# A three-stage encoder layer in one kernel: units in their own order, and products that accumulate in PSUM with copies in place of sums

## The chip, the cores and the metric

The kernel runs on one core of one Trainium2 chip. The metric is the device time of one execution in microseconds (us); the number given for a kernel is the median of its runs. A difference of 0.2% (3.9 us) is about what a measurement of this kernel can tell from no change.

## The reference

One encoder layer is applied to a prompt (1024 rows of 1024) and to a sample (512 rows), with the same weights, all in float32.

```python
h = _rmsnorm(x, norm_g)
proj = jnp.einsum('bld,de->ble', h, w_in)
(q, f_fw, f_bw, i, z_a, c_B, c_C, c_x, z_b, g_a, g_b) = jnp.split(proj, SPLIT_POINTS, axis=-1)
o_a = _hgrn2_bidir(q, i, f_fw, f_bw, lb_fw, lb_bw, hnorm_g).astype(x.dtype)
p_a = jnp.einsum('ble,ed->bld', o_a * jax.nn.silu(z_a), w_a)
conv = _centred_short_conv(c_C * c_x, conv_w, conv_b)
p_b = jnp.einsum('ble,ed->bld', c_B * conv * jax.nn.silu(z_b), w_b)
merged = jax.nn.sigmoid(g_a) * p_a + jax.nn.sigmoid(g_b) * p_b
return x + jnp.einsum('bld,de->ble', merged, w_o)
```

A final RMSNorm follows. `_hgrn2_bidir` is a gated linear recurrence over 8 heads of 128, run in both directions, and each of the 11 parts of `proj` is 1024 wide.

## The kernel before, in words

Every float32 operand is split into a high part (ScalarE, "ACT": `s_h`, `w_h`, L63) and a low part (VectorE, "DVE": `s_l`, `w_l`, L64), and each product is three matmuls, high x high, low x high and high x low. Nearly all matmuls on TensorE ("PE") are 128x128 by 128x512.

The stages follow each other in time:

1. Norm and values, to about 109 us.
2. The prompt's projection (L307), to about 872 us. It uses a Strassen-Winograd scheme: a product of 2x2 blocks with seven block products B11, T1, T2, T3, T4, B21, B22 in place of eight, and sums of blocks before and after.
3. The heads, to about 1514 us. The recurrence of each head is done in many small matmuls, and the sample's projections stand between them as *units* of 24 wide matmuls each (L77; a few are L70), so that PE has work while ACT and DVE prepare the small ones. What is left of the units runs to 1580 us.
4. Branch b, from 1580 us: prompt (L823, 336 matmuls), then sample (L77, 192). Branch a from 1709 us, likewise. Each uses the Strassen-Winograd products again, four blocks of 256 output columns for the prompt.
5. The output product from 1825 us (L823, 504 matmuls in six blocks) with the final norm, to the end.

In stage 3 the loop runs over 3 iterations per head: the two halves of the prompt and the sample. In an iteration the *previous* item gets near scores (L450), transposed keys (L499, into the banks "u" of PSUM, of which there are three, copied out by ACT), scores (L450, L484) and contributions (L512, also into "u" banks, copied out by ACT in L513); the current one gets its decays (L434 to L437, a chain between ACT and DVE). When all parts of a group have their contributions, `states` combines them on DVE (L521), `outputs` multiplies them with the queries (L536), and `finish` transposes the result (L550, "u" banks again) and multiplies it with a gate on DVE (L551). The order of the engines is that in which this code is written; it is kept as it is on PE, DVE, ACT and on the SyncE queue ("SP"), which issues all DMAs.

In stages 4 and 5 `two_blocks` makes one block of 256 output rows: `Rows` loads two 512 KB pieces of weights (`w_raw`), `sums` makes the sums S on DVE and splits them into the five buffers `w_h`, `w_l`, and `prod` runs one of the seven products, 12 matmuls into a PSUM bank of its own. DVE adds the products up in SBUF (`plus`, L827), adds a product to the sum and multiplies with the gate `s` (in branch a it also adds branch b's result, `pb`), and stores the result. The gates, `pb` tiles, and the raw operand pieces that `operands` loads (L724) share the pool `io` of seven 512 KB places. The last two operands, B21 and B22, are loaded by `last()`, four pieces for k = 0 to 3, each split twice on ACT and twice on DVE.

The memory of `cs`, a pool on the right side that holds what the heads need, is given to `wk` (S, sums, final gains) only when `order_pe` has closed, behind the last unit.

## Time and profile before

| | |
|---|---|
| median of 3 runs | 1956.26 us (1956.11 to 1957.43) |
| profiled execution | 1956.1 us, span 1954.2 us |
| busy | PE 1918.1 us (98%), DVE 1461.1 us (75%), ACT 940.2 us (48%) |
| matmuls in the trace | 14772 |

The span is the time from the first to the last instruction in the trace. Busy time is summed per engine. A wait is put down to the instruction or DMA that ended it. A wide matmul's row has a duration of 0.39 us, but such matmuls overlap: they start some 0.23 us apart.

### The profile page before, as it was taken

Reading aid. Unit: us, or ns where it says so; the run is one execution under the profiler, and the core shown is the slowest. Engines: PE = TensorE matmul, PEld = TensorE weight load, DVE = VectorE, ACT = ScalarE, POOL = GpSimd, SP = SyncE. Lnnn points to the kernel's source line nnn. Section 1 sums busy time; section 2 is a strip of 40 time slices with the busy share of each in tenths; the row PEclk is TensorE's granted clock in tenths of the full one; section 3 lists DMA queues with packets and bytes.
Section 4 is the critical chain, followed back from the end, with each engine's and each line's share of the span. In section 5 each row is a group of like instructions: output and inputs, shape, how many; then the busy total and the mean of one; then the engine's idle time right before and its main releaser. Section 6 shows DMA issues by size and latency. Waiting matters only on the chain.

```text
span 1954.2 us, 38023 instructions
## 1 busy us (share of the span) xinstructions
PE 1918.1 (98%) x14772; PEld 1615.2 (83%) x14772; DVE 1461.1 (75%) x2423; ACT 940.2 (48%) x1946; POOL 135.8 (7%) x220
## 2 busy tenths in 40 slices
PE   8999999999999999999999999999999999999998
PEld 8988888888888888887888888888888878888786
DVE  6558787878787878785677578878773557899887
ACT  6433443434444343434677577677674333434432
POOL 1000000000000000002122011122110000000000
PEclk8999999999999999999999999999999999999999
DMA  7466676676676767668555655555544965879852
GB/s 214 124 211 236 230 234 235 229 237 226 226 247 217 247 223 245 224 218 318 218 209 189 224 179 198 199 190 205 181 162 159 328 215 189 291 238 304 281 162 86
DMA packets 306436, 427.35 MB, mean 219 GB/s; under 512 B 26192, under 2 KB 178000, under 8 KB 306256
## 3 DMA queue, kind: packets, MB, share of 16 engines
q1 hardware_dynamic: 306256, 424.93, 63.7%
q8 instruction: 116, 1.90, 0.4%
q14 instruction: 64, 0.52, 0.1%
HBM read 254.98 MB, written 169.87 MB: 217 GB/s over the span
## 4 chain that ended last, share of the span: by engine, by line
PE 79%; DVE 8%; ACT 6%; issue 3%; DMA 3%; POOL 1%; SPq 0%; DVEq 0%; POOLq 0%; ACTq 0%
PE pp L307 39%; PE pw L823 13%; PE pp L77 12%; PE pp L201 5%; PE pw L77 3%; PE pp L70 2%; DVE K L436 2%; PE o L536 1%; ACT cat L435 1%; PE sc L450 1%; ACT cat L434 1%; DVE Q L437 1%; PE u L512 1%; POOL rs_o L81 1%; ACT oz L544 1%
## 5 line engine op out<-in xcount | busy, mean ns | idle before, releaser
L307 PE MATMUL pp<-s_h,w_h 128*128 128x512 f32 x1120 | 436.3, 390 | 1.2 <-ACT w_h L63 1.2
L307 PE MATMUL pp<-s_l,w_h 128*128 128x512 f32 x1120 | 436.2, 389 | 0.0
L307 PE MATMUL pp<-s_h,w_l 128*128 128x512 f32 x1120 | 436.2, 389 | 0.0
L77 PE MATMUL pp<-s_h,w_h 128*128 128x512 f32 x632 | 252.5, 400 | 1.2 <-ACT K L132 0.9
L63 ACT ACTIVATE w_h<-w_raw 128x512 fp32r<-128x512 f32 (+1 forms) x204 | 141.3, 693 | 226.4 <-PE pp L307 154.8
L307 PEld LDWEIGHTS pp<-s_h,w_h 128*128 128x128 f32 x1120 | 210.3, 188 | 45.3 <-ACT w_h L63 1.8
L77 PE MATMUL pp<-s_h,w_l 128*128 128x512 f32 x632 | 247.0, 391 | 0.0
L77 PE MATMUL pp<-s_l,w_h 128*128 128x512 f32 x632 | 246.5, 390 | 0.0
L307 PEld LDWEIGHTS pp<-s_h,w_l 128*128 128x128 f32 x1120 | 210.3, 188 | 43.6
L312 DVE TENSOR_TENSOR tmp<-pp,tmp 128x512 f32<-128x512 f32 x240 | 165.3, 689 | 108.2 <-PE pp L307 107.1
L307 PEld LDWEIGHTS pp<-s_l,w_h 128*128 128x128 f32 x1120 | 210.3, 188 | 43.4
L63 ACT ACTIVATE w_h<-w_S 128x512 fp32r<-128x512 f32 x160 | 99.5, 629 | 188.7 <-PE pp L307 85.9
L64 DVE TENSOR_TENSOR w_l<-w_raw,w_h 128x512 fp32r<-128x512 f32 (+1 forms) x204 | 155.7, 764 | 36.0 <-ACT w_h L63 35.7
L823 PE MATMUL pw<-s_h,w_h 128*128 128x512 f32 x392 | 154.1, 393 | 5.5 <-ACT w_h L63 5.5
L823 PE MATMUL pw<-s_h,w_l 128*128 128x512 f32 x392 | 154.4, 394 | 1.8 <-DVE w_l L64 1.8
L823 PE MATMUL pw<-s_l,w_h 128*128 128x512 f32 x392 | 154.0, 393 | 0.0
L434 ACT COPY cat<-K 128x512 f32<-128x512 f32 x168 | 112.2, 668 | 65.8 <-DVE K L436 36.2
L77 PEld LDWEIGHTS pp<-s_h,w_l 128*128 128x128 f32 x632 | 118.7, 188 | 25.5
L77 PEld LDWEIGHTS pp<-s_h,w_h 128*128 128x128 f32 x632 | 118.9, 188 | 24.5 <-ACT K L132 1.3
L77 PEld LDWEIGHTS pp<-s_l,w_h 128*128 128x128 f32 x632 | 119.0, 188 | 22.9
L436 DVE TENSOR_TENSOR K<-K,T 128x512 f32<-128x512 f32 x144 | 110.7, 768 | 30.7 <-ACT cat L434 27.7
L435 ACT COPY cat<-Q 128x512 f32<-128x512 f32 x168 | 112.3, 668 | 39.6 <-DVE Q L437 20.0
(188 smaller groups left out, 3288.0 us busy)
## 6 DMA issues: line engine op xcount, KB each, us to landing
w_raw<-in_w_in SPq DMA_DIRECT2D x80, 512.0 KB, 5.2
ws_d<-w_h SPq DMA_DIRECT2D x160, 256.0 KB, 2.4
ws_d<-w_l SPq DMA_DIRECT2D x160, 256.0 KB, 2.5
w_h<-ws_d SPq DMA_DIRECT2D x79, 512.0 KB, 4.3
w_l<-ws_d SPq DMA_DIRECT2D x79, 512.0 KB, 5.3
fkq_d<-sg SPq DMA_DIRECT2D x48, 256.0 KB, 2.3
v_raw<-in_w_in SPq DMA_DIRECT2D x32, 256.0 KB, 3.4
fkq_d<-sk SPq DMA_DIRECT2D x32, 256.0 KB, 2.4
```

The source lines that it names most:

```text
L63: A.activation(hi, src, AF.Copy)
L64: V.tensor_tensor(lo, src, hi.bitcast(F32), op=ALU.subtract)
L70: T.matmul(out, lhs(k, a), parts[k // 2][b][:, k % 2, :], start=k == 0 and n == 0, stop=k == KT - 1 and n == 2)
L77: T.matmul(out, whl[a][:, k, :], rhs(k, b), start=k == 0 and n == 0, stop=k == KT - 1 and n == 2)
L81: G.tensor_tensor(r, t, neghalf[:, :t.shape[-1]], op=ALU.pow)
L201: T.matmul(pp, B[f"B{k // 4 + 1}{t + 1}"][a][:, k % 4, c * P:(c + 1) * P], parts[k][b], start=k == 0 and m == 0, stop=k == KT - 1 and m == 2)
L307: T.matmul(bank, hl[x][:, k, :], B[b][y][:, k, :], start=k == 0 and i == 0, stop=k == 3 and i == 2)
L312: V.tensor_tensor(out, p, t, op=ALU.add)
L434: A.copy(ap(cat, 0, [[2 * hs, nb], [hs, 2], [1, hs]]), kall)
L435: A.copy(ap(cat, TB, [[2 * hs, nb], [hs, 2], [1, hs]]), qall)
L436: V.tensor_tensor(kall, kall, ap(t, m + 1, [[2, nb], [-m - 1, 2], [0, hs]]), op=ALU.mult)
L823: T.matmul(bank, hl[x][:, c:c + P], O[n][y][:, k, :], start=k == 0 and i == 0, stop=k == 3 and i == 2)
```

## The change

In stage 3 the units are in another order: for each head q, ff, fb, za, cx, cC, cB, zb, and all of gb and ga at the end. `finish` of the prompt and of the sample moves to the third iteration of the next head, around the scores; the sample's `outputs` moves to the second iteration behind contributions and a unit; two units stand at the end of the third iteration and one less in the second.

In stages 4 and 5 a product can continue the bank of an earlier one. B11, T2, T3 and T4 accumulate in one bank, T1 and B22 in another, B21 has its own. ACT copies the bank out three times on the way (c11, u2, u3); what was summed in SBUF is now summed in PSUM, and DVE has 56 additions less, ACT 28 copies more. The next block's B11 is made before the current block's products are done (`begun`), and in the first block `last()`, which loads the operands for B21 and B22, comes behind the next block's `Rows` and B11. `w_raw` has a pool of its own, `rp`; `cs` closes with the heads, and gates of left-over units go to `io`. In the changed file L500, L513, L537, L551, L552 are the former L499, L512, L536, L550, L551, and L730, L901, L904, L935 the former L724, L883, L886, L916.

```diff
         p0st.close()
+        rp = outer.enter_context(tc.tile_pool(name="rp", bufs=1, side="right", reuse_waits="tile"))
         cs = right.enter_context(tc.tile_pool(name="cs", bufs=1, side="right", reuse_waits="tile"))
         wp = st.enter_context(tc.tile_pool(name="wpp", bufs=1, side="right", reuse_waits="tile"))
...
-                ahead = [cs.tile([P, 1024], F32R, name=f"a_{x}") for x in "hl"]
+                ahead = [rp.tile([P, 1024], F32, name="w_raw", bufs=2) for _ in range(2)]
                 for a, z in enumerate(ahead):
-                    load(z.rearrange("p (k c) -> p k c", c=P).bitcast(F32), ws_d[SPLIT["q"], a])
+                    load(z.rearrange("p (k c) -> p k c", c=P), ws_d[SPLIT["q"], a])
...
+        gate_tile = lambda: cs.tile([P, TB], F32, name="sg", bufs=2)
...
-                s = cp.tile([P, TB], F32, name="sg", bufs=2)
+                s = gate_tile()
...
-        later = [narrow(n, h) for h in range(NH) for n in ("cx", "cC", "cB", "zb", "gb")]
-        later.insert(8, wide(1))
-        later += [narrow("ga", h) for h in range(NH)]
         units = []
         for h in range(NH):
-            units += [narrow(n, h) for n in ("q", "ff", "fb", "za")] + [wide(0)] * (h == 0) + later[4 * h:4 * h + 4]
-        units += later[4 * NH:]
+            units += [narrow(n, h) for n in ("q", "ff", "fb", "za")]
+            units += [wide(h // 2)] * (h in (0, 2)) + [narrow(n, h) for n in ("cx", "cC", "cB", "zb")]
+        units += [narrow(n, h) for n in ("gb", "ga") for h in range(NH)]
...
-        prev, to_output, to_finish = None, None, None
+        prev = None
         for i in range(len(order) + 1):
+            h, m = divmod(i, 3)
...
             if prev:
                 near_scores(prev)
                 transpose_keys(prev)
-            if to_output:
-                outputs(to_output, 0)
+            if m == 0 and h:
+                outputs(groups[h - 1], 0)
             if cur:
                 decays(cur)
                 if cur.b == 0:
                     values(cur.g)
-                    if cur.g.n == 8:
-                        cur.g.zg = gtile("zgp", [2 * TB])
-                        load(cur.g.zg, zg_d[cur.g.h])
             unit()
+            if m == 2 and h:
+                finish(groups[h - 1])
             if prev:
                 scores(prev)
+            if m == 2:
+                if h:
+                    finish(sample[h - 1].g)
+                groups[h].zg = gtile("zgp", [2 * TB])
+                load(groups[h].zg, zg_d[h])
+            if prev:
                 contributions(prev)
             unit()
-            if to_finish:
-                finish(to_finish)
-            if to_output:
-                outputs(to_output, 1)
-            if i % 3 < 2:
+            if m == 0 and h:
+                outputs(groups[h - 1], 1)
+            if m == 1 and h:
+                outputs(sample[h - 1].g, 0)
+            if m != 1:
                 unit()
-            to_finish, to_output = to_output, None
             if prev and len(prev.g.done) == len(prev.g.tbs):
-                to_output = prev.g
                 states(prev.g)
             prev = cur
+        outputs(sample[NH - 1].g, 0)
         unit()
-        outputs(to_output, 0)
-        if to_finish:
-            finish(to_finish)
-        unit()
-        finish(to_output)
+        finish(groups[NH - 1])
+        finish(sample[NH - 1].g)
         left.close()
+        right.close()
 
 
 
 
         qp, io = opened(outer, "qp", bufs=1), opened(outer, "io", bufs=7)
         ps = opened(outer, "psc", bufs=1, space=PSUM)
+        wk = opened(outer, "wk", bufs=1, side="right")
+        gate_tile = lambda: io.tile([P, TB], F32, name="io")
...
         def raw_block(src):
-            raw = io.tile([P, 1024], F32, name="w_raw", bufs=2)
+            raw = rp.tile([P, 1024], F32, name="w_raw", bufs=2)
...
-        def products(O, r, srcs, use):
-
-
-
+        def products(O, last, r, srcs, use):
+
+
+            def prod(hl, half, n, bank=None):
+                start = bank is None
+                if start:
+                    bank = ps.tile([P, TB], F32, name="pw", bufs=5)
+                for k in range(4):
+                    for i, (a, b) in enumerate(PASSES):
+                        c = half * TB + k * P
+                        T.matmul(bank, hl[a][:, c:c + P], O[n][b][:, k, :],
+                                 start=start and k == 0 and i == 0, stop=k == 3 and i == 2, skip_group_check=True)
+                return bank
+
+            def copied(bank):
+                c = wk.tile([P, TB], F32, name="c", bufs=6)
+                A.copy(c, bank)
+                return c
+
+            def begun(r):
+                r.x = prod(r.f, 0, "B11")
+                r.c11 = copied(r.x)
+
+            begun(r)
             i = 0
             while r.raws:
-                r = two_blocks(O, r, partial(use, i), i > 0, partial(srcs, i + 1))
+                if i:
+                    r.sums(0)
+                    r.sums(1)
+                ahead = Rows(srcs(i + 1))
+                if i == 0:
+                    y = prod(r.s12, 0, "T1")
+                prod(r.s12, 1, "T2", r.x)
+                u2 = copied(r.x)
+                if i == 0:
+                    ahead.first()
+                    begun(ahead)
+                    last()
+                else:
+                    y = prod(r.s12, 0, "T1")
+                prod(r.s34, 0, "T3", r.x)
+                u3 = copied(r.x)
+                use(i, 0, 0, prod(r.f, 1, "B21"), r.c11)
+                use(i, 1, 1, y, u3)
+                prod(r.last, 0, "T4", r.x)
+                use(i, 1, 0, r.x, None)
+                if i and ahead.raws:
+                    ahead.first()
+                    begun(ahead)
+                prod(r.s34, 1, "B22", y)
+                use(i, 0, 1, y, u2)
+                r = ahead
                 i += 1
-
-        def two_blocks(O, r, use, early, later):
-            def prod(hl, half, n):
-                bank = ps.tile([P, TB], F32, name="pw", bufs=5)
-                for k in range(4):
-                    for i, (x, y) in enumerate(PASSES):
-                        c = half * TB + k * P
-                        T.matmul(bank, hl[x][:, c:c + P], O[n][y][:, k, :], start=k == 0 and i == 0, stop=k == 3 and i == 2)
-                return bank
-
-            def plus(out, p, t):
-                V.tensor_tensor(out, p, t, op=ALU.add)
-
-            c11, c12, c21 = (wk.tile([P, TB], F32, name="c", bufs=6) for _ in range(3))
-            if early:
-                r.first()
-            A.copy(c11, prod(r.f, 0, "B11"))
-            if early:
-                use(0, 0, c11, prod(r.f, 1, "B21"))
-                r.sums(0)
-            plus(c12, prod(r.s12, 1, "T2"), c11)
-            if early:
-                r.sums(1)
-            ahead = Rows(later())
-            plus(c21, prod(r.s34, 0, "T3"), c12)
-            p5 = prod(r.s12, 0, "T1")
-            plus(c12, p5, c12)
-            use(1, 1, c21, p5)
-            use(1, 0, c21, prod(r.last, 0, "T4"))
-            if not early:
-                use(0, 0, c11, prod(r.f, 1, "B21"))
-            use(0, 1, c12, prod(r.s34, 1, "B22"))
...
-            def use(i, m, t, c, more):
+            def use(i, m, t, u, more):
                 m += 2 * i
-                u = wk.tile([P, TB], F32, name="sum", bufs=2)
-                V.tensor_tensor(u, more, c, op=ALU.add)
+                if more is not None:
+                    V.tensor_tensor(more, u, more, op=ALU.add)
+                    u = more
                 finish_block(m, t, s[m], u)
...
             r = prepared(srcs)
-            products(last(), r, srcs, use)
...
             def block(m, t, s, u):
-                V.tensor_tensor(u, u, s[:, t, :], op=ALU.mult)
-                V.tensor_tensor(s[:, t, :], u, pb[m][:, t, :], op=ALU.add)
+                V.tensor_tensor(s[:, t, :], u, s[:, t, :], op=ALU.mult)
+                V.tensor_tensor(s[:, t, :], s[:, t, :], pb[m][:, t, :], op=ALU.add)
...
                 V.tensor_tensor(x, c, x, op=ALU.add)
-                V.tensor_tensor(x, more, x, op=ALU.add)
+                if more is not None:
+                    V.tensor_tensor(x, more, x, op=ALU.add)
...
         order_pe.close()
-        right.close()
-        wk = opened(outer, "wk", bufs=1, side="right")
         fg = wk.tile([P, D], F32, name="fg")
         load(fg, w["final_g"].to_broadcast([P, D]))
-        branch_b_prompt(lambda: last_operands(O, take(0, 1), rows))
+        branch_b_prompt(O, lambda: last_operands(O, take(0, 1), rows))
```

PE in the third iteration of a head and the beginning of the next, before: L512 are the contributions that complete the prompt's group, L550 the transposes of the sample's finish, L536 the prompt's outputs. The rows left out are the 24 wide matmuls of one unit.

```order
L512 MATMUL u<-v_11694,kT 128x128 x7
...
L550 MATMUL u<-ident,oz 128x128 x4
L450 MATMUL sc<-q,kd 32x32 x16
L450 MATMUL sc<-cat 32x32 x48
L499 MATMUL u<-ident,K 128x128 x6
L536 MATMUL o<-v_11694,pt 128x128
L536 MATMUL o<-us_12173,Q 128x128
```

The same place after; the first gap is one unit, the second two.

```order
L500 MATMUL u<-ident,K 128x128 x7
...
L551 MATMUL u<-ident,oz 128x128 x8
L451 MATMUL sc<-cat 32x32 x48
L485 MATMUL sc<-cat 64x64 x8
L551 MATMUL u<-ident,oz 128x128 x4
L513 MATMUL u<-v_11697,kT 128x128 x7
...
L451 MATMUL sc<-q,kd 32x32 x16
L451 MATMUL sc<-cat 32x32 x48
L500 MATMUL u<-ident,K 128x128 x6
L537 MATMUL o<-v_11697,pt 128x128
L537 MATMUL o<-us_12152,Q 128x128
```

A second unit has come between contributions and outputs, all twelve transposes of the finishes have moved ahead of the contributions, and before them the eight stand behind a unit of their own.

The SyncE queue at the start of branch a, before: L724 loads the pieces of oz_p for B21 and B22, L883 and L886 load gates and pb tiles (here those of block 0 and the first of block 1), L762 loads weights, L916 stores a finished tile.

```order
L886 DMA io_18637<-pb_p_77 128x1024 [waits DMAHW5_49,DMAHW3_49]
L883 DMA io_18639<-sga_p_81 128x1024 [waits DMAHW6_49,DVE_49]
L886 DMA io_18641<-pb_p_77 128x1024 [waits DMAHW0_49,DVE_49]
L724 DMA io_18668<-oz_p_75 128x1024 [waits DMAHW7_49,DMAHW2_49]
...
L724 DMA io_18674<-oz_p_75 128x1024 [waits DMAHW5_49,DMAHW3_49]
L724 DMA io_18680<-oz_p_75 128x1024 [waits DMAHW2_49,DVE_49]
L724 DMA io_18686<-oz_p_75 128x1024 [waits DMAHW6_49,DMAHW0_49]
L883 DMA io_18727<-sga_p_81 128x1024 [waits DMAHW5_49,DMAHW1_49,DVE_49]
...
L916 DMA m_p_79<-io_18639 128x1024
```

After: L901 and L904 load gates and pb tiles, L935 stores a finished tile, L730 loads the pieces of oz_p.

```order
L904 DMA io_18648<-pb_p_77 128x1024 [waits DMAHW5_49,DMAHW3_49]
...
L901 DMA io_18650<-sga_p_81 128x1024 [waits DMAHW6_49]
L768 DMA w_raw_18809<-in_w_a 128x8x128 [waits DMAHW0_49,DMAHW1_49,DVE_49,Activation_49]
L904 DMA io_18652<-pb_p_77 128x1024 [waits DVE_49]
L935 DMA m_p_79<-io_18602 128x1024 [waits DMAHW2_49]
L730 DMA io_18704<-oz_p_75 128x1024 [waits DMAHW2_49]
L730 DMA io_18710<-oz_p_75 128x1024 [waits DMAHW4_49,DMAHW3_49,DVE_49]
L730 DMA io_18716<-oz_p_75 128x1024 [waits DMAHW5_49,DMAHW4_49,DVE_49]
L768 DMA w_raw_18811<-in_w_a 128x8x128 [waits DVE_49]
L730 DMA io_18722<-oz_p_75 128x1024 [waits DMAHW7_49,DMAHW5_49,DVE_49]
```

The loads of oz_p stood ahead of block 1's gates and of every store; now they stand behind all eight tiles of blocks 0 and 1 and behind the first store.

DVE ahead of branch b, before: S are the sums of block 0's weights; the splits `s_l` of operands are those that run along the last units and, the eight of them, those of B21 and B22.

```order
L64 TENSOR_TENSOR s_l<-io,s_h 128x512 x2
L64 TENSOR_TENSOR w_l<-w_raw,w_h 128x1024
L64 TENSOR_TENSOR s_l<-io,s_h 128x512 x8
L793 TENSOR_TENSOR S<-w_raw 128x512
L789 TENSOR_TENSOR S<-w_raw 128x512
L794 TENSOR_TENSOR S<-S,w_raw 128x512
```

After, where L552 is the last gate multiplication of the heads.

```order
L552 TENSOR_TENSOR oz<-u,zg 128x512
L799 TENSOR_TENSOR S<-w_raw 128x512
L795 TENSOR_TENSOR S<-w_raw 128x512
L800 TENSOR_TENSOR S<-S,w_raw 128x512
L796 TENSOR_TENSOR S<-w_raw,S 128x512
L64 TENSOR_TENSOR s_l<-io,s_h 128x512
```

The sums have moved from behind the operands' splits to the end of the heads.

## Rows read from the trace of the kernel before

**Rows 1.** The page, busy time of each engine, share of the span and instructions.

```profile
PE 1918.1 (98%) x14772; PEld 1615.2 (83%) x14772; DVE 1461.1 (75%) x2423; ACT 940.2 (48%) x1946; POOL 135.8 (7%) x220
```

**Rows 2.** Windows by stage: us, busy time (instructions) by engine, PEclk, DMA share, GB/s.

```profile
core 0: us, PE busy (x) PEld busy (x) DVE busy (x) ACT busy (x) POOL busy (x), PEclk, DMA share, GB/s
...
872.00:1514.00 642.00, 628.29 (x8718) 532.48 (x8717) 445.27 (x802) 417.76 (x1070) 118.81 (x192) 1.00 0.57 204
...
1580.00:1709.00 129.00, 124.66 (x543) 102.42 (x543) 103.82 (x149) 48.24 (x66) 0.00 (x0) 0.99 0.71 231
1709.00:1825.00 116.00, 116.00 (x513) 96.14 (x512) 105.01 (x156) 42.35 (x58) 0.00 (x0) 1.00 0.83 274
```

**Rows 3.** Waits of PE: engine, line, what for; us in total, times, longest us.

```profile
PE pw L823 <- ACT w_h L63: 5.5, 3, 4.0
PE u L550 <- ACT us L513: 5.4, 4, 1.7
PE o L536 <- DVE us L521: 4.3, 6, 1.6
```

**Rows 4.** Timeline, PE from 955 to 968: start, us, form, xcount [wait].

```profile
955.18 1.06 PE L450 MATMUL sc<-cat 128*32 128x32 f32 x96
956.17 0.69 PE L484 MATMUL sc<-cat 128*64 128x64 f32 x16
...
966.00 0.39 PE L536 MATMUL o<-v,pt 128*128 128x128 f32 x2
967.21 0.49 PE L536 MATMUL o<-us,Q 128*128 128x128 f32 x2 [0.82 <-DVE us L521]
967.53 0.39 PE L536 MATMUL o<-v,pt 128*128 128x128 f32 x2
```

**Rows 5.** Timeline from 1306 to 1313, PE's and DVE's part of a finish.

```profile
1306.59 0.60 PE L550 MATMUL u<-ident,oz 128*128 128x128 f32 x4
...
1308.88 0.66 PE L550 MATMUL u<-ident,oz 128*128 128x128 f32 x4 [1.69 <-ACT us L513]
...
1309.29 0.48 PE L77 MATMUL pp<-s_h,w_h 128*128 128x512 f32 x1
...
1309.60 0.40 PE L77 MATMUL pp<-s_l,w_h 128*128 128x512 f32 x1
...
1312.16 1.27 DVE L551 TENSOR_TENSOR oz<-u,zgp 128x512 f32<-128x512 f32 x2
```

**Rows 6.** Timeline from 1582 to 1592, the start of branch b.

```profile
1582.54 0.39 PE L823 MATMUL pw<-s_h,w_l 128*128 128x512 f32 x1
...
1583.86 0.69 DVE L793 TENSOR_TENSOR S<-w_raw 128x512 f32<-128x512 f32 x1
...
1591.52 0.39 PE L823 MATMUL pw<-s_h,w_l 128*128 128x512 f32 x1
```

**Rows 7.** Tile oz_p from 1690 to 1760: issues on SyncE, first and last start.

```profile
L724 SPq DMA_DIRECT2D io<-oz_p x4: 319/320/320, 1702.8 to 1713.7; - x4
...
DMA to landing us min/median/max: 3.3/4.4/5.4
```

**Rows 8.** Tile m_p from 1690 to 1790, the stores of L916.

```profile
DMA to landing us min/median/max: 3.3/5.1/7.0
```

**Rows 9.** Timeline from 1831 to 1836, the start of the output stage.

```profile
1831.25 0.50 PE L823 MATMUL pw<-s_h,w_h 128*128 128x512 f32 x1 [1.02 <-ACT w_h L63]
...
1834.12 0.61 ACT L63 ACTIVATE w_h<-w_raw 128x512 fp32r<-128x512 f32 x1
1834.18 0.69 DVE L945 TENSOR_TENSOR io<-c,io 128x512 f32<-128x512 f32 x1
1834.79 1.22 DVE L64 TENSOR_TENSOR w_l<-S,w_h 128x1024 fp32r<-128x1024 f32 x1
1835.92 0.69 DVE L64 TENSOR_TENSOR w_l<-w_raw,w_h 128x512 fp32r<-128x512 f32 x1
```

**Rows 10.** Timeline of the end; the last matmul starts at 1945.75.

```profile
1947.27 0.68 DVE L946 TENSOR_TENSOR io<-pw,io 128x512 f32<-128x512 f32 x1
```

More of the change, by code (lines that the diff above doesn't have):

```diff
@@ L587, in prepare @@
                 if (name, h) == ("q", 0):
-                    return [z.rearrange("p (k c) -> p k c", c=P) for z in ahead]
+                    return [z.rearrange("p (k c) -> p k c", c=P).bitcast(F32R) for z in ahead]
                 return parts_from(ws_d[SPLIT[name] + h], (KT, P))
@@ L871, in branch_b_sample, with branch_prompt @@
                 store(pb_x[1][j], s)
-        def branch_prompt(name, last, finish_block, pb=None):
+        def branch_prompt(name, O, last, finish_block, pb=None):
             s = {}
@@ L886, in srcs, with branch_b_prompt @@
                         load(pb[j].rearrange("p a b -> p (a b)"), pb_x[0][j])
[L888 removed]
+            def use(i, m, t, u, more):
                 m += 2 * i
[L890 to L891 removed]
+                if more is not None:
+                    V.tensor_tensor(more, u, more, op=ALU.add)
+                    u = more
                 finish_block(m, t, s[m], u)
             r = prepared(srcs)
[L895 to L897 removed]
+            products(O, last, r, srcs, use)
+        def branch_b_prompt(O, last):
             left_of = {}
@@ L904, in block, with branch_a_prompt @@
                     store(pb_x[0][m], s.rearrange("p a b -> p (a b)"))
-            branch_prompt("w_b", last, block)
-        def branch_a_prompt(last):
+            branch_prompt("w_b", O, last, block)
+        def branch_a_prompt(O, last):
             pb = {}
             def block(m, t, s, u):
-                V.tensor_tensor(u, u, s[:, t, :], op=ALU.mult)
-                V.tensor_tensor(s[:, t, :], u, pb[m][:, t, :], op=ALU.add)
+                V.tensor_tensor(s[:, t, :], u, s[:, t, :], op=ALU.mult)
+                V.tensor_tensor(s[:, t, :], s[:, t, :], pb[m][:, t, :], op=ALU.add)
                 left_of[m] = left_of.get(m, 0) + 1
@@ L918, in branch_a_prompt @@
             left_of = {}
-            branch_prompt("w_a", last, block, pb)
+            branch_prompt("w_a", O, last, block, pb)
         def branch_a_sample(blocks, act):
@@ L929, in branch_a_sample, with output @@
                 store(m_x[1][j], s)
-        def output(last):
+        def output(O, last):
             xt, ss, halves = {}, {}, {}
@@ L957, in output @@
             r = prepared(srcs)
-            products(last(), r, srcs, use)
+            products(O, last, r, srcs, use)
         FIRST, LAST = ("B11", "T1", "T2", "T3", "T4"), ("B21", "B22")
@@ L994, in trunk_kernel @@
         branch_b_sample(blocks, act)
-        branch_a_prompt(lambda: last_operands(O, take(2, 4), rows))
+        branch_a_prompt(O, lambda: last_operands(O, take(2, 4), rows))
         rows = lambda k: w["w_o"][k * P:(k + 1) * P, :]
@@ L1002, in trunk_kernel @@
         branch_a_sample(blocks, act)
-        output(lambda: last_operands(O, take(5, 6), rows))
+        output(O, lambda: last_operands(O, take(5, 6), rows))
 def _masks():
```

5 lines of the change are left out of this document (1 added, 4 removed).

## Prediction

> **What bounds the kernel now.** The page comes first: TensorE (PE) is busy for 1918.1 of 1954.2 us [rows 1], so the time is a fixed stream of matmuls plus the holes in it. The windows by stage say where the holes are: 13.7 us in the 642 us of the heads stage, 4.3 us at branch_b's prompt part, none from 1709 to 1825, where 513 wide matmuls take 116.00 us, 0.226 us each [rows 2]. PE's own waits name what ends the holes [rows 3]. Every term below is therefore a hole that closes or opens on PE; the 56 additions that leave VectorE (DVE) count only where PE waits for DVE. The profiled execution is 1956.1 us against a median of 1956.26, so the sum is made on 1956.1 and needs no correction.
>
> **The heads stage, what closes.** Six times the prompt outputs (L536) wait for the states that L521 makes, 4.3 us in all [rows 3]. Before, one unit of 24 wide matmuls, the last four transposes of a finish, and the near scores and key transposes stand between the contributions (L512) and these outputs; after, two units and no transposes. One unit more is 24 x 0.226 = 5.4 us, and the longest wait is 1.6 us, so all six should go. Four times the second half of the eight output transposes (L550) waits for a "u" bank that ScalarE (ACT) empties with L513, 5.4 us in all; at 1308.88 PE stands for 1.69 us for the copies of the contributions just ahead [rows 3, 5]. After, the eight transposes stand a whole unit behind the key transposes, and the banks that they take were emptied before or are being emptied by two short copies during that unit. A stop costs a little more than its wait: the step from 966.00 to 967.21 is 1.21 us, the next one 0.32, an excess of 0.89 for a wait of 0.82 [rows 4]. Ten stops at about 0.1 each make it 4.3 + 5.4 + 1.0 = 10.7 us.
>
> **The heads stage, what opens.** After, the contributions (L513) follow the transposes closely and take two banks that now hold transposed outputs, until DVE has multiplied them with the gate (0.64 us each, two in 1.27 [rows 5]). Between the eight transposes and the contributions PE has 48 + 8 score products and four more transposes: 0.99 (955.18 to 956.17), 0.69 and 0.60 at most [rows 4, 5], some 2.2 us less overlaps. If DVE is free, the first product is done 0.64 us behind the first four transposes and nothing waits; DVE may be about 1.9 us late. What DVE has queued ahead there is the decay chain of the next block, which the key copies and six cat copies on ACT pace, and the wide unit in between (5.4 us) covers nearly all of it. Before, PE found DVE late by up to 1.6 us at the states [rows 3]. I put 1.5 us on the seven places together; nothing and 10 us are the ends (0 or 1.4 us each). Seven fewer changes from small to wide matmuls, 0.09 us each (1309.29 to 1309.60 is such a first step, 0.31 against 0.23 [rows 5]), give 0.6 us back.
>
> **branch_b's start.** From the matmul at 1582.54 to that at 1591.52 there are twelve steps, which take 8.98 us instead of 2.72: 6.3 us are lost [rows 6]. Most is one hole right behind 1582.54: the sums S could start only at 1583.86, because their space was the gate pool's, which closed with the last gate. Some steps behind the hole are slower, which the 6.3 us include. After, the pool closes with the heads, DVE makes S some 66 us before it is needed, and all weights that the first three products take are split while the last units run. B21 and B22 now come from operands loaded behind the last gate's store, of which the fourth waits for the first's space: 1 us for that (0.3 to 2). So 6.3 - 1.0 = 5.3 us close.
>
> **branch_a's start, where a hole opens.** Here the order on the SyncE queue decides. Before, the four loads of oz_p that feed B21 and B22 are issued from 1702.8 to 1713.7 [rows 7], and PE has no hole from 1709 on [rows 2]. After, blocks 0 and 1 both ask for their gate and pb tiles first: 8 tiles, and the io pool has 7. The eighth (L904) waits until DVE has finished block 0's first tile, and the oz_p loads stand behind it. Six of the seven places then hold tiles that need B21 or B22 or block 1, so the four loads go one after the other through one place: each waits for the four splits of the one before it, and the first waits for the store of the finished tile.
>
> The times, from branch_a's first matmul: T4 ends after 76 matmuls, at 17.2 us; a multiplication and an addition on DVE (0.69 each when alone [rows 9]) make 18.6, the eighth load and the store's issue 19.3. A store of m_p lands after 5.1 us in the median, a load of oz_p after 4.4 [rows 7, 8]: 24.4 and 28.8. The first split ends at 29.4 (0.61 on ACT [rows 9]); PE, which has eight products to do first, has been waiting since 96 x 0.226 = 21.7, so a hole of 7.7 us. Two splits on ACT and one more on DVE end 2.0 us after a landing, so each of the next three rounds lasts 6.4 us: the last piece lands at 48.0 and its last split ends at 50.0. (Between the splits of the third and the fourth piece DVE has seven other operations, 6 x 0.61 + 1.13 = 4.8 us back to back [rows 9]; these just fit beside the load.) A PE without holes would be there after 168 matmuls, at 38.1: 11.9 us. Behind the last hole some steps are slow. At branch_b the twelve steps lose 6.3 us, of which the long wait is 4.0 [rows 3]; of the other 2.3, a second wait and the slow steps, I take 1.4 for the steps and add it once. It also covers DVE's queue, 13 operations (8.5 us) ahead of a split that PE takes 33 matmuls (7.5 us) later. I take 13.3 us. The ends come from the shortest and longest of these transfers (3.3 and 3.3; 7.0 and 5.4 [rows 7, 8]). With 3.3 the third piece's last split ends at 38.5, DVE's seven operations and the last two splits follow, and 44.6 is 6.5 behind, 7.9 with the slow steps; with 7.0 and rounds of 7.4 it is 55.9, 19.2. After the block the stream is as dense as before and nothing gives this back.
>
> The Trainium skill (DMA: Bandwidth & Descriptors, "Anatomy of one DMA — SWDGE (gpsimd) path") has a DMA cost about 2.0 us plus its bytes at 436 GB/s, fitted to DMAs that GpSimd issues, which for 512 KB is an estimate of 3.2 us. By it the hole would be about the small end, and the time about 1950; the medians of this trace are 4.4 and 5.1, and only its shortest transfers agree.
>
> **The rest of the products.** In the steady state each bank rests for at least one product (12 x 0.226 = 2.7 us) for the ACT copy (a pass over 128x512 takes ACT 0.61 [rows 9]) and for the next weights' split; nothing opens. The output stage starts with the same wait for m_p's rows; one more sum on DVE stands ahead of the one whose split PE awaits at 1831.25 [rows 9], and the next block's B11 comes a little before its rows: 0.6 us (0 to 2). At the end two additions follow the last product instead of one (1947.27 [rows 10]): 0.6 us.
>
> **The sum.** -10.7 + 1.5 - 0.6 - 5.3 + 13.3 + 0.6 + 0.6 = -0.6 us: 1955.5 us.
>
> **The rivals.**
> 1. The hole at branch_a is short: the queues are nearly empty while PE stands still, so each transfer takes 3.3 us. For it: the shortest rows; against it: the loads of weights for block 2 and the stores of block 0 fall in the same stretch. The hole is 7.9, the time 1950.1; with no new wait in the heads, 1948.6. Faster.
> 2. The contributions in the heads wait for DVE: place, the first L513 behind each finish; it opens from a lateness of 1.9 us on, and with 1.4 us at seven places the time is 1955.5 - 1.5 + 10 = 1964; from 0.9 us each on it is slower. For it: DVE is at 445 of 642 us in that stage and the order gives one iteration a unit less than it had [rows 2]; against it: the iteration that was shortest before was shorter still. Slower. The long end of branch_a's hole (19.2) alone gives 1961.4.
> 3. The states stay late although the outputs come 5 us later, because the gate multiplications now stand ahead of them on DVE, so the change does not do what it does on paper there: +4.3 to +5, 1960.
>
> **How the numbers follow.** A measurement of this kernel can tell 0.2%, 3.9 us, from no change: faster is below 1952.3, slower above 1960.2. My forecast holds with 0.42, rival 1 with 0.33, rival 2 or the long hole with 0.17, rival 3 with 0.08, half of it on either side of 1960.2. So faster 0.33, same 0.46, slower 0.21. The range runs from 1948, just beyond rival 1 with clean heads, to 1963, nearly to rival 2; the likeliest case alone is 1952 to 1960.
>
> **What would show it.** In the profile after: no wait of the outputs for states and none of the transposes for ACT's copies; the heads stage 8 to 11 us shorter; no hole at branch_b's first T product; at branch_a the oz_p loads issued one by one, 5 to 7 us apart, from about 24 us behind its first matmul, and four holes on PE ended by their splits, the first near 7 us, 8 to 19 in sum; the clock below full in that stretch. The prediction is wrong if those loads are issued earlier, if PE finds other products to do meanwhile, or if the heads stage gets holes at L513.

## The result, and the profile after

The changed kernel takes 1977.01 us in the median of four runs (1974.79 to 1978.62), the kernel before 1956.19 beside it: a ratio of 1.0104 (95% interval 1.0091 to 1.0116). The profiled execution of the changed kernel has a span of 1975.6 us, 21.3 more than the one of before. The forecast was 1955.5 with a range to 1963, so it was wrong.

The page after, busy time of each engine, which answers to [rows 1]:

```profile
PE 1927.0 (98%) x14772; PEld 1622.2 (82%) x14772; DVE 1431.5 (72%) x2367; ACT 957.4 (48%) x1974; POOL 142.8 (7%) x220
```

DVE has its 56 instructions less and ACT its 28 more; the work on PE is the same 14772 matmuls, 7032 of them wide ones of 128x128 by 128x512. Where the 21.3 us are is seen when the span is cut at the first matmul of each stage. The heads run here from the end of the prompt's projection to branch b's first matmul. "Output" reaches from its first matmul to the end; a wait of that first matmul counts to branch a's sample part.

| us | before | after | difference | predicted |
|---|---|---|---|---|
| heads and left-over units | 697.86 | 710.63 | +12.8 | -9.8 |
| branch b, prompt | 82.44 | 76.20 | -6.2 | -5.3 |
| branch a, prompt | 76.16 | 88.82 | +12.7 | +13.3 |
| branch a, sample | 44.17 | 46.25 | +2.1 | +0.6, the output's first wait |
| output to the end | 127.90 | 128.18 | +0.3 | +0.6, the tail |

What is left, 43.5 us of branch b's sample part and the stages before the heads, differs by under 0.5. The two large terms behind the heads came within 1 us. The heads alone are off by 22.6.

Waits of PE after; columns as in [rows 3].

```profile
PE u L513 <- DVE oz L552: 14.1, 7, 2.4
PE pw L824 <- ACT s_h L63: 5.6, 2, 5.3
PE pw L824 <- ACT w_h L63: 3.8, 2, 2.6
...
PE u L513 <- ACT us L514: 2.5, 1, 2.5
```

The two waits of [rows 3] that were to close, transposes for ACT (5.4) and outputs for states (4.3), are gone from the list. In their place the contributions (L513) stand seven times for DVE's gate multiplication (L552), 2.0 us each, and once for ACT's own copy.

The window of the heads, as in [rows 2]:

```profile
872.00:1514.00 642.00, 621.97 (x8648) 529.02 (x8647) 449.40 (x805) 414.89 (x1053) 126.96 (x191) 0.98 0.57 199
```

In a stretch of the same length PE is busy 6.3 us less and makes 70 matmuls fewer, and its mean granted clock has gone from 1.00 to 0.98 of 2.4 GHz. DVE and ACT are busy within 1% of what they were. So nothing is busier; somebody is late. One of the seven places, on the timeline from 1100 to 1116:

```profile
1100.18 1.23 DVE L417 SCALAR_TENSOR_TENSOR Q<-q,F 128x1024 f32<-128x1024 f32 x1 [17.06 <-PE o L537]
...
1101.60 1.39 POOL L81 TENSOR_TENSOR rs_o<-sso,neghalf 128x4 f32<-128x4 f32 x1 [21.92 <-DVE sso L542]
...
1103.02 1.14 ACT L545 ACTIVATE oz<-o,rs_o 128x128 f32<-128x128 f32 x4 [1.12 <-POOL rs_o L81]
...
1104.04 0.29 ACT L459 ACTIVATE near<-sc 128x128 f32<-128x128 f32 x1
...
1105.03 0.92 ACT L436 COPY cat<-Q 128x512 f32<-128x512 f32 x1
...
1107.64 1.03 PE L551 MATMUL u<-ident,oz 128*128 128x128 f32 x8
...
1111.95 1.28 DVE L552 TENSOR_TENSOR oz<-u,zgp 128x512 f32<-128x512 f32 x2
...
1112.69 2.04 PE L513 MATMUL u<-v,kT 128*128 128x128 f32 x14 [1.82 <-DVE oz L552]
```

The transposed outputs are in their banks from 1108.7 on, but DVE takes them only at 1111.95: the decay chain (L437, L438) stands ahead on it. The chain is late because it passes back and forth between DVE and ACT, and ACT, from 1101.19 to 1104.04, copies one piece of it, stands 1.12 us for GpSimd's `rs_o` and then scales four outputs. It also began late: the place that it needs for `Q` came back only with the sample's outputs (17.06 us idle on DVE, ended by L537). At the other six places DVE stands less than 0.8 us there, while ACT stands 1.1 to 1.7 us for `rs_o` at all seven. Two suspects, then: ACT's wait for GpSimd, and the late return of `Q`.

Branch a's start. SyncE's timeline from 1722 to 1756, loads of weights left out:

```profile
1731.25 0.32 SPq L904 DMA_DIRECT2D io<-pb_p  x1
1731.62 0.43 SPq L935 DMA_DIRECT2D m_p<-io  x1
1736.74 11.99 SPq L730 DMA_DIRECT2D io<-oz_p  x3
...
1753.58 0.32 SPq L730 DMA_DIRECT2D io<-oz_p  x1
```

The tile oz_p from 1700 to 1760, from issue to landing:

```profile
DMA to landing us min/median/max: 3.1/3.2/4.5
```

PE's timeline from 1733 to 1755, its waits for splits of these pieces:

```profile
1740.59 0.80 PE L824 MATMUL pw<-s_h,w_h 128*128 128x512 f32 x1 [5.32 <-ACT s_h L63]
...
1747.11 0.73 PE L824 MATMUL pw<-s_h,w_h 128*128 128x512 f32 x2 [0.32 <-ACT s_h L63]
```

Before, the four loads were issued from 1702.8 to 1713.7, around the first matmul of that part [rows 2, 7]. Now the first goes out 24.4 us behind branch a's first matmul (1712.30), the second at 1741.89, the third at 1748.42: one by one, 5 to 6.5 us apart.

### The profile page after: what moved, and what is told of

Read it like the earlier page. It is cut to its first block, busy times and chain, and to the rows that moved or that the text cites. A ratio compares the mean times of both kernels' runs of the same rounds, so it can differ in the third digit from the quotient of the medians.

```text
span 1975.6 us, 37915 instructions
## 1 busy us (share of the span) xinstructions
PE 1927.0 (98%) x14772; PEld 1622.2 (82%) x14772; DVE 1431.5 (72%) x2367; ACT 957.4 (48%) x1974; POOL 142.8 (7%) x220
## 4 chain that ended last, share of the span: by engine, by line
PE 80%; DVE 7%; ACT 4%; issue 4%; DMA 4%; POOL 1%; SPq 0%; DVEq 0%; POOLq 0%; ACTq 0%
PE pp L308 39%; PE pp L77 16%; PE pw L824 11%; PE pp L201 5%; PE pw L77 2%; DVE Q L438 2%; PE o L537 2%; PE u L513 2%; ACT cat L436 1%; PE sc L451 1%; DVE K L437 1%; DMA io<-in_w_o 1%; DMA w_raw<-in_w_a 1%; POOL rs_o L81 1%; ACT oz L545 1%
## 5 line engine op out<-in xcount | busy, mean ns | idle before, releaser
L308 PEld LDWEIGHTS pp<-s_l,w_h 128*128 128x128 f32 x1120 | 210.2, 188 | 43.5
L438 DVE TENSOR_TENSOR Q<-Q,T 128x512 f32<-128x512 f32 x144 | 111.2, 772 | 27.1 <-ACT cat L436 25.3
```

Of the source, the lines that this page charges most:

```text
L308: T.matmul(bank, hl[x][:, k, :], B[b][y][:, k, :], start=k == 0 and i == 0, stop=k == 3 and i == 2)
L438: V.tensor_tensor(qall, qall, ap(t, 1, [[2, nb], [m - 1, 2], [0, hs]]), op=ALU.mult)
```

## The experiments

Each run is timed beside the kernel before on the same chip; ratios are to that kernel, with 95% intervals. The table cuts their profiled executions as above.

| us | heads | branch b | branch a | a, sample | output | median | ratio |
|---|---|---|---|---|---|---|---|
| e1_fourth_q | 699.8 | 76.2 | 88.3 | 45.1 | 127.6 | 1966.44 | 1.0041 (1.0026 to 1.0056) |
| e2_outputs_back | 688.2 | 76.2 | 88.3 | 46.0 | 127.1 | 1955.70 | 0.9990 (0.9980 to 0.9999) |
| e3_last_first | 711.2 | 76.4 | 82.8 | 43.5 | 126.6 | 1968.15 | 1.0057 (1.0039 to 1.0074) |
| e4_loop_before | 694.2 | 76.2 | 88.4 | 47.7 | 127.8 | 1961.23 | 1.0018 (1.0009 to 1.0027) |
| e5_both_mended | 688.0 | 76.4 | 81.4 | 43.5 | 128.4 | 1944.57 | 0.9931 (0.9914 to 0.9947) |
| e6_fourth_q_no_rs | 684.5 | 76.2 | 88.7 | 47.8 | 127.9 | 1950.47 | 0.9965 (0.9952 to 0.9978) |
| e7_no_rs_three_q | 684.5 | 76.2 | 88.5 | 46.8 | 128.4 | 1951.73 | 0.9976 (0.9967 to 0.9985) |
| e8_sums_in_sbuf | 688.9 | 76.2 | 76.2 | 43.8 | 127.6 | 1940.60 | 0.9913 (0.9898 to 0.9928) |
| e9_first_block_sums | 688.0 | 76.2 | 76.3 | 43.5 | 131.8 | 1942.61 | 0.9923 (0.9910 to 0.9937) |
| e10_late_scaling | 684.9 | 76.2 | 88.3 | 46.1 | 128.2 | 1951.42 | 0.9972 (0.9961 to 0.9983) |
| e11_sums_late_scaling | 706.1 | 76.2 | 76.2 | 46.1 | 127.3 | 1962.91 | 1.0024 (1.0014 to 1.0033) |
| e12_sums_decays_first | 684.8 | 76.2 | 76.2 | 46.3 | 127.5 | 1937.07 | 0.9892 (0.9874 to 0.9910) |

**e1: a fourth place for Q.**

```diff
-            k.Q = Q = gtile("Q", [2, TB], 3)
+            k.Q = Q = gtile("Q", [2, TB], 4)
```

> One edit in the changed kernel: the scaled queries Q get a fourth place in place of three. Theory A (the decay chain of the sample cannot begin before the sample's outputs of the head before have given back its Q, and these outputs now stand at the end of the second iteration; the gate multiplications stand behind that chain on VectorE, and the contributions wait for them): VectorE no longer stands still in the second iteration, the waits of L513 for L552 fall from 14.1 us to below 3, and with the slow steps behind them the time falls by 15 to 22 us, to 1955 to 1962. Theory B (the chain between VectorE and ScalarE is simply longer than the cover, wherever it begins): the waits stay above 8 us and the time above 1971. Theory C (ScalarE is late, since the outputs' normalisation and its wait for GpSimd stand ahead of the chain's copies): as B, since the order on ScalarE is not touched.

Some of the loss goes (heads -10.8), but PE still waits for L552, 11.0 us in five waits: more than theory A has, and the time lies between the bands. ACT now stands longer for GpSimd at such a place: its row at 1169.01 waits 3.91 us for `rs_o`. What the fourth place changes isn't shown: DVE still stands 15.21 us for L537 ahead of L417 at 1094.6.

**e2: the sample's outputs back at the start of the iteration.**

```diff
+            if m == 1 and h:
+                outputs(sample[h - 1].g, 0)
             if cur:
                 decays(cur)
...
-            if m == 1 and h:
-                outputs(sample[h - 1].g, 0)
```

> One edit in the changed kernel: the sample's outputs go back to where they were in the second iteration, right behind the transposed keys, still in the iteration before the finish. Theory A (Q's place): Q is given back early again, the waits of L513 for L552 fall below 3 us, the time to 1955 to 1962. Theory B (the chain is too long in any case): waits above 8 us, time above 1971. Theory C (ScalarE late through the outputs' normalisation): falls like A, so that this run and the one with a fourth Q tell A and C apart together.

The heads take 9.7 us less than before, where the prediction's terms for them sum to 9.8, and the waits at L513 are 2.2 us in five, where it had put 1.5 on seven:

```profile
PE u L513 <- DVE oz L552: 2.2, 5, 0.7
```

So all of the heads' loss comes from the new place of one step, and what else is new there does what it was forecast to do. The move takes back both suspects at once.

**e3: B21's and B22's loads ahead of the next block's.**

```diff
+                if i == 0:
+                    last()
                 ahead = Rows(srcs(i + 1))
...
                     begun(ahead)
-                    last()
```

> One edit in the changed kernel: in each first block the loads of the operands for B21 and B22 are asked for before block 1's rows, gates and pb tiles, as in the kernel before. The theory that the eight gate tiles in seven places cause branch_a's hole: branch_a's prompt part takes 76 to 78 us in place of 88.8, and the time falls by 11 to 13 us, to 1964 to 1966. Rival (the hole comes from the new order of the products, which needs B21 early): it stays above 6 us and the time above 1970.

Neither side of the expectation is met. Branch a gains 6.0 us, not the whole 12.7, and a new wait of PE for ACT's copy (c, L830) of 4.9 us appears.

**e4: the loop of before, the new order of the units.** The heads' loop is that of the diff's minus lines; all else stays changed.

> The changed kernel with the heads' loop of the kernel before (outputs, finish and the number of units in their old places); the new order of the units and all of the products stay. If the whole loss of the heads stage (12.8 us) comes from the loop: the heads stage is as long as before to within 2 us and the time is 1963 to 1966. If the order of the units costs something by itself, the time is above 1968.

The heads take 694.2, 3.7 less than before and 16.5 less than after: neither the units' order nor the pools cost anything there; the loop does. Heads and time are a little below what was expected.

**e5: e2, with `last()` ahead of the block's first product.**

```diff
+            last()
             begun(r)
...
                     begun(ahead)
-                    last()
```

> The changed kernel with the sample's outputs back behind the transposed keys and, in each first block, the operands for B21 and B22 asked for before the first product. If branch_a's hole comes from the queue for the seven places alone: branch_a's prompt part takes 76 to 77 us in place of 88.3, the output stage starts 2 us sooner too, and the time is 1940 to 1943, below both kernels. Rival (the early use of B21 and the copies on ScalarE make a hole by themselves, as the 82.8 us with the loads merely moved ahead of block 1 suggest): branch_a stays above 80 us and the time above 1946.

Branch a still lacks 5.2 us, and the time lies between the bands of the two theories. What is there, on the timeline of e5 from 1694 to 1700:

```profile
1694.20 0.63 ACT L63 ACTIVATE s_h<-io 128x512 fp32r<-128x512 f32 x1 [4.87 <-DMA io<-oz_p]
...
1698.20 1.15 ACT L63 ACTIVATE s_h<-io 128x512 fp32r<-128x512 f32 x2 [1.90 <-DMA io<-oz_p]
...
1699.26 0.56 ACT L830 COPY c<-pw 128x512 f32<-128x512 f32 x1
...
1699.88 0.50 PE L824 MATMUL pw<-s_h,w_h 128*128 128x512 f32 x1 [3.28 <-ACT c L830]
```

B11 was done near 1694, and T2, which continues its bank, could have started at 1696.4. The copy of the bank stands on ACT behind splits that stand for loads.

**e6 and e7: ACT doesn't wait for GpSimd.** Both leave out the scale by `rs_o`; e6 has four places for Q, e7 three.

```diff
-                    A.activation(oz[:, c, :], p[:, c, :], AF.Copy, scale=r[:, c:c + 1])
+                    A.activation(oz[:, c, :], p[:, c, :], AF.Copy, scale=1.0)
```

> The changed kernel with a fourth place for Q, and the recurrence's outputs are copied without their scale (the normalisation by rs_o is left out of the copy, so that ScalarE does not wait for GpSimd there; GpSimd still makes it). Theory C for what the fourth Q left (ScalarE stands for GpSimd's rs_o with the key copies and the chain's copies behind it): the waits of L513 for L552 fall from 11.0 to below 3 us, the heads from 699.8 to 688 to 692, the time to 1955 to 1959. Theory B (the chain is too long by itself): the waits stay above 7 us and the time above 1963.

> The changed kernel with three places for Q as it has, and the outputs copied without their scale (as in the run with a fourth Q and no scale, the normalisation is left out of the copy). If both causes lie one behind the other: the waits of L513 for L552 fall from 14.1 to 4 to 10 us, the heads from 710.6 to 695 to 704. If Q's place alone set the chain's start, they stay above 12 us; if the scale alone did, they fall below 3 us and the heads to 690.

Both take 684.5 us in the heads, and neither has a wait at L513. This is less than e6 was expected to reach, and e7 refutes what I held by then, that both causes act in series: with ACT free, the late Q costs nothing.

**e8: e5 with the products of before.** `products`, `two_blocks` and branch a's and b's sums are those of the diff's minus lines, with `last()` ahead of the first product; the wider pools of the change stay.

> The changed kernel with the sample's outputs back behind the transposed keys, and with the products of the kernel before (each in a bank of its own, sums on VectorE in SBUF, operands loaded first); the early closing of the gate pool stays. If the accumulation in PSUM gives PE nothing and branch_b's gain is that of the early closing: branch_b's prompt part takes 76 to 77 us, branch_a's 76 to 77, and the time is 1940 to 1945. If the accumulation or the earlier B11 is what closed branch_b's hole: branch_b takes above 79 us.

Branch a is back at 76.16, and on ACT the same copy of B11 stands in the same place (at 1698.64, behind four splits); here T2 has a bank of its own, and nobody waits for it. Branch b is as fast without accumulation, and the tail behind the last matmul's start is 8.49 us again instead of 9.21.

**e9: e5, but the first block adds up on DVE.**

```diff
-                prod(r.s12, 1, "T2", r.x)
-                u2 = copied(r.x)
                 if i == 0:
+                    u2 = plus(prod(r.s12, 1, "T2"), r.c11)
                     ahead.first()
                     begun(ahead)
+                    p = prod(r.s34, 0, "T3")
+                    u3, more = plus(p, u2), plus(p, u2)
...
```

> As e5_both_mended, but in the first block of each stage T2, T3 and T4 get banks of their own and DVE adds them up, so that no product of that block waits for ACT's copy of B11; T1 and B22 still share a bank, and all later blocks accumulate as before. If branch_a's remaining 5.2 us are the wait of T2 for that copy, which stands on ACT behind the splits of B21's and B22's first two pieces, branch_a's prompt part is 76.2 to 77.0 us, PE has no wait there for ACT c L830, and the time is 1939.5 to 1941.5. If accumulation costs something else (banks, the order of the next block's B11), branch_a stays at 79 to 82 and the time above 1942.5. What the later blocks' accumulation is worth is this time less that of e8_sums_in_sbuf (1940.6): 0 to +1 by the theory, the longer tail alone.

Branch a takes 76.3, so its 5.2 us were T2's wait for the copy with the slow steps behind it. The total is 1.1 above that theory's band and 2.0 above e8: in the output stage a hole of 3.2 us opens, where the next block's B11, now the fourth product, waits for the split of rows that have just landed:

```profile
1823.14 1.06 ACT L63 ACTIVATE w_h<-w_raw 128x1024 fp32r<-128x1024 f32 x1 [1.45 <-DMA w_raw<-m_p]
...
1824.25 0.79 PE L824 MATMUL pw<-s_h,w_h 128*128 128x512 f32 x1 [3.24 <-ACT w_h L63]
```

**e10: after, with the sample's scaling copies behind the next decays.** Nothing is left out, and Q comes back as late as in the changed kernel. The sample's copies are kept in a list and written later; the prompt's stay where they were:

```diff
-                for c in range(CPB):
-                    A.activation(oz[:, c, :], p[:, c, :], AF.Copy, scale=r[:, c:c + 1])
+                waiting.append((oz, p, r))
...
                     values(cur.g)
+            scaled()
             unit()
```

> The changed kernel, with the sample's outputs in their new place, but ACT's four scaling copies of those outputs (the ones that stand for GpSimd) are written behind the next iteration's decays, among the key copies and the chain. Nothing is left out. Q comes back as late as in the changed kernel. If ACT standing for GpSimd ahead of the key copies and the chain is the cause, the heads take 684 to 689 us and the time is 1950 to 1955, with under 3 us of waits at L513's line. If Q's late return or the place itself is the cause, the heads stay above 700 and the time above 1965. If the scaled outputs now come late for their transposes, a wait of the finish's transposes for ACT opens instead, 1 to 2 us at seven places, 1958 to 1965.

The heads take 684.9. The same place as above, on the timeline from 1093 to 1106 (L551, L558 and L559 are the former L545, L551 and L552):

```profile
1093.10 1.22 DVE L417 SCALAR_TENSOR_TENSOR Q<-q,F 128x1024 f32<-128x1024 f32 x1 [17.06 <-PE o L537]
...
1094.69 0.90 ACT L436 COPY cat<-Q 128x512 f32<-128x512 f32 x1
1095.46 0.31 ACT L459 ACTIVATE near<-sc 128x128 f32<-128x128 f32 x1
1095.94 0.37 ACT L551 ACTIVATE oz<-o,rs_o 128x128 f32<-128x128 f32 x1 [0.17 <-POOL rs_o L81]
...
1100.56 1.03 PE L558 MATMUL u<-ident,oz 128*128 128x128 f32 x8
...
1102.34 1.28 DVE L559 TENSOR_TENSOR oz<-u,zgp 128x512 f32<-128x512 f32 x2
...
1103.62 1.73 PE L513 MATMUL u<-v,kT 128*128 128x128 f32 x14
```

Counted from L417, which waits the same 17.06 us, the transposes start after 7.46 us in both kernels. But the chain's first copy of Q now runs at 1.6 instead of 4.85, DVE is at the gate after 9.24 instead of 11.77, and L513 has no wait. In the whole run one is left at that line:

```profile
PE u L513 <- DVE oz L559: 0.4, 1, 0.4
```

**e11 and e12: the best of both.** Both are e8 with the sample's outputs at the changed kernel's place. In e12 the sample's copies are written as in e10. In e11 the prompt's are moved too, and the sample's are written just behind the key transposes, ahead of the decays; its expectation below describes them wrongly.

> e8_sums_in_sbuf with the sample's outputs back in the place of the changed kernel and all scaling copies on ACT, the prompt's too, behind the decays. By the theory the heads come down from 688.9 to the 684.5 that they took without the scale, and the time from 1940.6 to 1936 (1935 to 1938). If the copies come late for the transposes of the finish, 1940 to 1945.

> e8_sums_in_sbuf with the sample's outputs in the changed kernel's place and its scaling copies behind the next iteration's decays, as in e10_late_scaling and unlike e11_sums_late_scaling, where two of the four copies still stood on ACT ahead of the copy of the near scores. By the theory it takes e10's heads (684.9) and e8's rest: 1940.6 - (688.9 - 684.9) = 1936.6 (1935 to 1939). If e10's gain depended on something other than ACT's order, the heads are 688 or more and the time 1940 or more.

e12 came out as expected, 1937.07 us, and has the lowest median of all; the 3.5 us to e8 are less than the 3.9 that a measurement can tell, but the heads go the same way (684.8 against 688.9). e11 lies 25 us above its range. ACT in e11 at such a place, from 1103 to 1106 (its line 551 is the changed kernel's L545):

```profile
1103.25 0.63 ACT L551 ACTIVATE oz<-o,rs_o 128x128 f32<-128x128 f32 x2 [1.12 <-POOL rs_o L81]
1103.76 0.28 ACT L459 ACTIVATE near<-sc 128x128 f32<-128x128 f32 x1
1103.92 0.38 ACT L551 ACTIVATE oz<-o,rs_o 128x128 f32<-128x128 f32 x1
1104.17 0.50 ACT L502 COPY kT<-u 128x384 f32<-128x384 f32 x1
1104.53 0.41 ACT L551 ACTIVATE oz<-o,rs_o 128x128 f32<-128x128 f32 x1
...
1105.26 0.92 ACT L436 COPY cat<-Q 128x512 f32<-128x512 f32 x1
```

Two of the four copies that stand for GpSimd are still ahead of the near scores' copy and all four ahead of the chain's first copy of Q, which in e10 goes before them. PE waits as in the changed kernel:

```profile
PE u L513 <- DVE oz L559: 14.5, 7, 2.9
```

So e11 points the same way, but since it also moves the prompt's copies, it doesn't test ACT's order alone.

## Why the prediction was wrong

**What failed is the term of +1.5 us for the contributions' wait: it measured 16.6 us (14.1 + 2.5), and with it failed the price of a stop, which was put at its wait and about 0.1 us.** The term rests on the sentence that DVE's queue ahead of L552 is the decay chain, that ACT's copies pace it, and that the unit in between "covers nearly all of it". The place, the number and the engine waited for were those of rival 2, which held 1.4 us at each of seven places as a bound; they are seven, of 2.0 us. The step that was left out is ACT's: I read the moved outputs as PE work that comes a unit later for the states, and did not cost the rest of what they issue. Each brings four squares, a power on GpSimd (1.39 us in the row at 1101.60) for which ACT stands, and four copies on ACT (1.14), and in the new place these stand at the end of one iteration, right ahead of the next one's key copies and chain. e7 and e10 tell this apart from Q's late return: free ACT of that wait, by leaving the scale out or by writing it later, and the loss is gone though Q comes back just as late. Why a fourth Q (e1) gives back 10.8 us stays open. The Trainium skill (PSUM — Partial Sum Buffer, "Engine vs sequencer instructions") calls the queues of ScalarE and VectorE strict FIFO; the rows from 1101.19 to 1105.03 agree, where the copies of the near scores and of Q go out only when the scaled outputs are through. The prediction weighed the order on DVE, not that on ACT.

The waits at L513 grew by 14.4 us against e2 (14.1 + 2.5 - 2.2), the heads by 22.5. The remaining 8 us are for the most part slow steps. In five stretches of the heads the granted clock was 0.50, that is 1.2 GHz in place of 2.4; the windows of these, columns as in [rows 2], and their sum:

```profile
1022.00:1028.80 6.80, 4.47 (x15) 3.90 (x16) 6.80 (x15) 5.44 (x13) 2.86 (x4) 0.50 0.21 68
1114.20:1117.60 3.40, 3.40 (x11) 2.72 (x11) 3.15 (x7) 3.30 (x9) 0.53 (x2) 0.50 1.02 262
1185.80:1189.20 3.40, 3.40 (x15) 3.17 (x15) 3.15 (x8) 2.60 (x7) 0.53 (x2) 0.51 0.88 276
1257.50:1260.90 3.40, 2.96 (x14) 2.96 (x15) 3.40 (x8) 2.29 (x6) 0.62 (x2) 0.50 0.44 155
1472.60:1476.00 3.40, 3.40 (x15) 3.21 (x15) 2.94 (x7) 2.60 (x7) 0.00 (x0) 0.50 0.90 283
sum 20.40, PE 17.63 PEld 15.96 DVE 19.44 ACT 16.23 POOL 4.54; mean PE 3.53 PEld 3.19 DVE 3.89 ACT 3.25 POOL 0.91
```

Half of PE's 17.63 us, 8.8, is an estimate of what the lower clock cost. Each of the five began in or just behind a stop of 1.8 to 2.4 us at L513; behind those of 1.27 us (to 1330.41) and 2.27 us (to 1401.45) the clock stayed at 1.00. Before, and in e2, e10 and e12, the heads are granted 1.00 throughout. e11 has two such stretches with 7.74 us of PE (3.9 by the same estimate); its heads are 21.3 us longer than those of e12, and 16.8 us of that are waits at L513.

**What held in the heads.** Both waits that were to close did (9.7 us in [rows 3]); e2 gives the whole sum without the moved step, -9.7 against -9.8. That this fits so closely is in part luck: e10, which has the moved step and 0.4 us of waits, comes to -13.0, where the terms without the wait sum to -11.3.

**Branch b: right.** -6.2 against -5.3; the sums S start at 1526.23, 66.4 us ahead of the first matmul at 1592.58. The 1 us that I took off for the late operands did not show. e8 has the same 76.2 without accumulation, so the gain is not that of accumulation. It fits the early closed pools, by the time at which S starts; no run keeps all else and closes them late.

**Branch a: right in cause; the sum came out by luck.** First load 24.4 us behind the first matmul (24 forecast), loads one by one, 12.7 us against 13.3. Its make-up was another. The transfers took 3.2 us in the median (4.4 assumed) and PE came to its wait 1.1 us later, so the first hole is 5.5 us for 7.7, and only one small one behind it (0.5) is ended by a split. In place of the two more that were forecast stand 2.6 us of slow steps behind the first hole (1.4 allowed; the granted clock was 0.50 from 1738.8 to 1745.6), 0.8 for ACT's copy of a bank, 0.8 for a multiplication on DVE and 1.4 for a split of weights on ACT; these are the excesses over 0.23 us of the steps between matmuls. The sum is right because shorter transfers and stops that were not forecast cancel. The Trainium skill (DMA: Bandwidth & Descriptors, "Anatomy of one DMA — SWDGE (gpsimd) path") has a fit for DMAs that GpSimd issues, by which a load of 512 KB is an estimate of 3.2 us. The median of these four, issued by SyncE, agrees. The hole was not as short as rival 1 has it: e3 and e5 show that with the loads mended there is another wait beneath, T2's for ACT's copy, worth 5.2 us (a step 3.5 us too long, the rest slow steps behind it).

**The rest of the products.** "In the steady state nothing opens" held: branch b takes 76.2 with accumulation and without. The tail is 0.72 us longer (0.6 forecast). Branch a's sample part with the output's first wait took 2.1 us more; that wait, 2.6 us here, is also there in e11 (2.4) and e12 (2.6), which have no hole in branch a, and is under 0.1 in e8, so what sets it stays open.

**Rival 3** (states stay late) is out: no wait of L537 for L521's successor is left.

## What to carry to other kernels

When a step moves, list what it issues on every engine, and look at what stands behind its slowest wait: a wait for a third engine at the end of an iteration delays the first thing that the next iteration needs, even on engines that are half idle. Accumulating in one bank makes the next product depend on the copy of the last one, so such a copy must not stand in a queue behind work that waits for loads; a sum on another engine has no such tie. Here the gains of the change came from two of its parts, the loop's order without the moved step and what was done to the pools: e8, which keeps these and drops the accumulation, takes 1940.6 us where the kernel before takes 1957.0. e12 has the moved step too, with its copies written later, which the change did not have: 1937.1.

## What the hardware showed that was not expected

- Seven waits of 2.0 us cost the heads more than 14 us, since behind five of them PE ran at a granted clock of 0.50. In e5 the matmuls behind a stop of 3.28 us start 0.43 us apart instead of 0.23, from 1700.8 to 1703.8; the granted clock from 1700.5 to 1703.9 was 0.50. Before, in branch b, it was 0.50 from 1587.3 to 1590.7, behind the stop of 4.0 us in [rows 3].
- GpSimd's power of 128x4 numbers takes 1.0 us in the median of 24 in the changed kernel, but 1.4 to 1.5 at the seven places and up to 1.98 in e1, about as long as ACT's four copies that wait for it (1.14).
- 512 KB loads issued one at a time landed in 3.2 us in the median; those of before, beside other traffic, in 4.4 [rows 7].
